# Decoder layer with product-key experts: dense blocks in another order, and the first eight expert groups' scores made ahead of the dense stage

## The chip, the core and the metric

The kernel is one program on one core of a Trainium2 chip. TensorE (PE) multiplies matrices into PSUM; VectorE (DVE), ScalarE (ACT) and GpSimd (POOL) work on SBUF tiles of 128 partitions; SyncE (SP) issues the plain transfers, POOL the gathers by index. Every engine works through its own instructions in a fixed order and waits on semaphores for the others. The time is the device time of one execution in microseconds (us); the median of three is quoted.

## The reference, cut to what matters

One decoder layer over 1024 tokens of 1024 features. The token mixers ahead of the feed-forward part are not touched by the change. What matters is the feed-forward part, a product-key layer with 16,384 experts of one row each: every token picks 16 of them in each of 8 heads.

```python
def peer_ffn(h, wq, k1, k2, u_tab, v_tab):
    q = (h @ wq)...                                  # 8 heads, two halves of 128
    s1, s2 = scores of the halves against 128 keys each
    v1, i1 = lax.top_k(s1, 16); v2, i2 = lax.top_k(s2, 16)
    top_s, pos = lax.top_k(sums of the pairs, 16)
    idx = i1 * 128 + i2 at pos                       # expert numbers
    gates = jax.nn.softmax(top_s, axis=-1)
    act = jax.nn.gelu(einsum('bthkd,btd', u_tab[idx], h))
    return einsum('bthk,bthkd->btd', gates * act, v_tab[idx])
...
h = layer_norm(ALPHA * h + peer_ffn(h) + sigmoid(h @ w_gate) * (p @ w_ple))
```

## The kernel before, in words

**Blocks.** The 1024 tokens are eight blocks of 128, worked on in three groups, `BLOCKS = [(0, 1), (2, 3, 4), (5, 6, 7)]`. The expert layer is computed in two ways. Blocks 0, 1, 2, 5 and 6 gather: for each of the 128 experts of a token POOL fetches a row of `u` and later one of `v` (128 rows, 512 KB, for the 128 tokens at a time) into one of six `vr` buffers, and DVE makes one product of it (class `Experts`; in the trace line L139, `vr<-vr,h1r` for `u`, `acc<-vr,w,acc` for `v`). That is 1,280 gathers and products in all. The blocks in `DENSE = (3, 4, 7)` are computed against all experts, in 128 groups of 128.

**The dense blocks.** `spread` turns the numbers and gates that `choose` found for one block into a table with a place for every expert: one-hot tiles `ohA` and `ohB` are made by DVE and ACT, four tokens at a time in 32 groups, PE multiplies them (L996), ACT copies the result into `stage`, and SP stores it in the DRAM table `Gd`. `dense` then takes the expert groups one by one. For each it needs two weight blocks of 512 KB, `uE` and `v`, which come through `stream` into eight buffers `wf`. `uE` is split by ACT and DVE into a high and a low half (`split`, tiles `hl`; DVE's part is L256), and PE makes the scores of three blocks, 384 columns, by 24 matmuls of halves (`mm`, L281 to L283: high by high, high by low, low by high, with `h1s` the split activations). ACT applies the Gelu and leaves `y` in one of seven buffers `cs`. DVE multiplies `y` by the gates in two halves (L1052), from tiles `gp` that SP loads from `Gd` for eight expert groups at a time, in two halves `c` of 768 KB (L1036): the 12 rows of `Gd` for a half are block after block, so `c = 0` is the first dense block and half of the second. Last, `back` (L1028) multiplies `y` by `v` and accumulates in six PSUM banks, `g` and `z`, over all expert groups; it is emitted one expert group behind the score.

**The order.** `main` emits the program by generators that tell how long each step takes, and `Merge` takes the one that is behind. In the last group of blocks `choose` of block 7, with its `spread`, is merged with `embed`; then `choose` of blocks 5 and 6 with `dense`. The gathers and their products are put between them at a rate. `choose` keeps its tables `top`, `cv` and `ci` in the same seven `cs` buffers as `y` and the one-hot tiles. From what is emitted a scheduler fixes each engine's instruction order when the program is built. On the chip each engine only follows it and waits.

```python
ex.rate = RATES["last"]
yield from Merge(choose(o, [t for t in o.tbs if t in DENSE]), embed(o))
ex.rate = RATES["dense"]
yield from Merge(choose(o, [t for t in o.tbs if t not in DENSE]), dense(h1s))
```

## Time and profile before

| | us |
|---|---|
| median of three runs | 3288.61 (3286.11 to 3297.98) |
| the profiled execution | 3287.69 |
| its span on the core | 3285.6 |
| PE busy | 2934.3 (89%) |
| DVE busy | 2626.9 (80%) |
| ACT busy | 1095.3 (33%) |
| POOL busy | 1581.4 (48%) |
| moved by the DMA engines | 1035.22 MB, mean 315 GB/s |

The profile records one execution: each instruction of each engine with its start and duration in us from the start of the span, the wait that came before it and what ended that wait, and the clock that was granted to PE in a stretch (1.0 is 2.4 GHz, 0.5 is 1.2 GHz). A row names the line of the kernel, the operation, and `out<-in` by the names of the tiles; `x8` is eight such instructions in a row. Matmuls are pipelined, so a row's duration reaches into the next one's. A whole fp32 matmul is two PE instructions in the trace, one row in an order of instructions.

### The profile page before, as it was taken

The page shows a single profiled execution, that of the slowest core. Times are in us where ns is not written, and L with a number is a line of the kernel's source. Part 1 is how long each engine was busy: PE and PEld are TensorE (multiplying, and loading weights), DVE is VectorE, ACT ScalarE, POOL GpSimd, SP SyncE. Part 2 cuts the span into 40 slices and gives each one's busy share as a digit, 9 for nine tenths or more (in the row PEclk, how much of TensorE's full clock was granted, in tenths as well). Part 3 has the DMA queues.
Part 4 walks back from the last instruction along what each step waited for, and adds up shares of the span by engine and source line. Part 5 has one row for each costly group of instructions (what it writes and reads, how often), then busy time and mean ns, then how long its engine had stood idle before and what let it go on. Part 6 is the DMA issues. An engine that isn't in the chain of part 4 may idle for free.

```text
span 3285.6 us, 39190 instructions
## 1 busy us (share of the span) xinstructions
PE 2934.3 (89%) x12265; PEld 2013.0 (61%) x12265; DVE 2626.9 (80%) x5567; ACT 1095.3 (33%) x2590; POOL 1581.4 (48%) x1313
## 2 busy tenths in 40 slices
PE   7997999969899937999898966999999999999990
PEld 6886655655464535667655554666666666666660
DVE  5535898788789999898887999976676677777788
ACT  5626335421621458556423154111111111111110
POOL 0000066667634544576674343545454555554564
PEclk9998999969999969999899988999999999999995
DMA  6344698989978979898899888999999999999997
GB/s 219 130 141 144 230 365 317 375 293 379 390 274 308 354 281 329 295 370 308 292 380 350 303 304 292 366 358 345 351 352 361 352 350 345 353 350 339 360 330 272
DMA packets 341824, 1035.22 MB, mean 315 GB/s; under 512 B 38512, under 2 KB 95216, under 8 KB 341616
## 3 DMA queue, kind: packets, MB, share of 16 engines
q0 software_dynamic: 184320, 671.17, 56.3%
q1 hardware_dynamic: 157296, 361.55, 30.3%
q8 instruction: 97, 1.59, 0.2%
q14 instruction: 111, 0.91, 0.1%
HBM read 991.17 MB, written 41.42 MB: 314 GB/s over the span
## 4 chain that ended last, share of the span: by engine, by line
PE 66%; DVE 15%; issue 7%; ACT 7%; DMA 3%; POOL 1%; SPq 0%; DVEq 0%; ACTq 0%; POOLq 0%
PE g L279 15%; PE g L1028 13%; PE z L1028 6%; PE m L283 5%; PE m L281 5%; PE m L282 5%; PE g L793 3%; DVE acc L139 3%; ACT ohB L161 2%; PE g L283 2%; PE g L281 2%; PE g L282 2%; PE m L617 2%; DVE vr L139 2%; PE z L590 1%
## 5 line engine op out<-in xcount | busy, mean ns | idle before, releaser
L1088 POOL DMA_INDIRECT vr<-in_u_dram,vidx x640 | 784.3, 1226 | 968.3 <-DVE V L139 385.7
L1088 POOL DMA_INDIRECT vr<-in_v_dram,vidx x640 | 793.4, 1240 | 706.9 <-DVE acc L139 297.6
L139 DVE SCALAR_TENSOR_TENSOR acc<-vr,w,acc 128x1024 f32<-128x1024 f32 x640 | 818.4, 1279 | 58.1 <-DMA vr<-in_v_dram,vidx 50.5
L139 DVE SCALAR_TENSOR_TENSOR vr<-vr,h1r 128x1024 f32<-128x1024 f32 x640 | 780.5, 1220 | 70.9 <-DMA vr<-in_u_dram,vidx 50.4
L1028 PE MATMUL g<-wf,y 128*128 128x512 f32 x1024 | 462.5, 594 | 16.6 <-DVE y L1052 16.6
L161 ACT ACTIVATE hl<-wf 128x512 fp32r<-128x512 f32 x256 | 161.7, 631 | 942.1 <-PE m L282 798.1
L256 DVE TENSOR_TENSOR hl<-wf,hl 128x512 fp32r<-128x512 f32 x256 | 178.9, 700 | 287.5 <-ACT hl L161 234.6
L281 PE MATMUL m<-h1s,hl 128*128 128x384 f32 x1024 | 393.8, 385 | 5.3 <-DVE gs L868 3.0
L283 PE MATMUL m<-h1s,hl 128*128 128x384 f32 x1024 | 347.7, 340 | 4.6 <-DVE hl L256 4.6
L282 PE MATMUL m<-h1s,hl 128*128 128x384 f32 x1024 | 345.6, 337 | 0.0
L279 PE MATMUL g<-hT,wf 128*128 128x384 f32 x1024 | 341.7, 489 | 3.2 <-DVE gs L860 3.2
L1028 PEld LDWEIGHTS g<-wf,y 128*128 128x128 f32 x1024 | 192.9, 190 | 203.8 <-issue 183.9
L279 PEld LDWEIGHTS g<-hT,wf 128*128 128x128 f32 x1024 | 192.4, 191 | 136.8 <-issue 9.8
L1028 PE MATMUL z<-wf,y 128*128 128x512 f32 x512 | 240.6, 592 | 0.0
L281 PEld LDWEIGHTS m<-h1s,hl 128*128 128x128 f32 x1024 | 193.8, 189 | 35.8 <-issue 29.7
L282 PEld LDWEIGHTS m<-h1s,hl 128*128 128x128 f32 x1024 | 193.8, 189 | 28.9 <-issue 28.9
L283 PEld LDWEIGHTS m<-h1s,hl 128*128 128x128 f32 x1024 | 193.5, 189 | 6.1 <-DVE hl L256 4.9
L996 PE MATMUL z<-ohA,ohB 128*128 128x128 f32 x768 | 137.2, 320 | 45.2 <-ACT ohB L161 19.6
L279 PE MATMUL g<-h1T,wf 128*128 128x384 f32 x512 | 173.0, 493 | 0.0
L1028 PEld LDWEIGHTS z<-wf,y 128*128 128x128 f32 x512 | 97.3, 190 | 122.4 <-issue 122.2
L996 PEld LDWEIGHTS z<-ohA,ohB 128*128 128x128 f32 x768 | 112.2, 211 | 71.8 <-ACT ohB L161 53.4
L256 DVE TENSOR_TENSOR wf<-wf 128x1024 fp32r<-128x1024 f32 x68 | 83.1, 1222 | 68.9 <-ACT wf L161 66.8
(336 smaller groups left out, 4606.5 us busy)
## 6 DMA issues: line engine op xcount, KB each, us to landing
wf<-in_uE_dram SPq DMA_DIRECT2D x128, 512.0 KB
wf<-in_v_dram SPq DMA_DIRECT2D x128, 512.0 KB
wf<-in_wmain_dram SPq DMA_DIRECT2D x84, 512.0 KB
wf<-in_wgate_dram SPq DMA_DIRECT2D x48, 512.0 KB
wf<-in_wq_dram SPq DMA_DIRECT2D x48, 512.0 KB
Gd<-stage SPq DMA_DIRECT2D x48, 512.0 KB
gp<-Gd SPq DMA_DIRECT2D x32, 768.0 KB
wf<-in_wout_dram SPq DMA_DIRECT2D x24, 512.0 KB
```

The source lines that it names most:

```text
L139: x = getattr(vec, op)(*args, **kw)
L161: x = nc.scalar.activation(o, i, f, **kw)
L256: vec.tensor_tensor(lo, src, hi, op=OP.subtract)
L279: pe.matmul(o, l[0], r[0], start=first, stop=last)
L281: pe.matmul(o, l[0], r[0], start=first, stop=False)
L282: pe.matmul(o, l[0], r[1], start=False, stop=False)
L283: pe.matmul(o, l[1], r[0], start=False, stop=last)
L617: pe.matmul(pw[:, c], sp[:, c], nident, start=False, stop=True, skip_group_check=True)
L793: pe.matmul(acc, yT[k // 4][:, k % 4, n * P:(n + 1) * P], wo[u][k // 2][:, k % 2, :], start=k == 0, stop=k == 7)
L996: pe.matmul(pg[:, k], B[:, k], A[:, k], start=True, stop=True)
L1028: pe.matmul(acc[d][c], y[:, d * P:(d + 1) * P], wv[:, c * 512:(c + 1) * 512], start=e == 0, stop=e == P - 1)
L1088: pool.indirect_dma_start(out=vr, out_offset=None, in_=use[0], in_offset=bass.IndirectOffsetOnAxis(ap=idx[:, s:s + 1], axis=0))
```

## The change

`DENSE` becomes `(7, 3, 4)`, so that the three dense blocks are contiguous columns (256 to 640) of the tile with the unsplit activations, `h1Ts`. A new generator `ahead` follows `embed`, and is thereby merged with `choose` and `spread` of block 7: for the first `NPRE = 8` expert groups it makes the scores by eight whole fp32 matmuls each, from the unsplit `uE` and `h1Ts`, and its Gelu goes into two buffers of four scores each (`yp`, one of the eight `c6` tiles, and a tile of the kind `vx`), in which they stay until `dense` multiplies them by the gates. `dense` makes its own scores from the ninth group on, split as before. The stream is ordered accordingly: eight `uE` unsplit, their eight `v`, then pairs. The `gp` tiles are taken when they are loaded, and the load for the groups 8 to 15 is taken apart: half 0 at the first group, half 1 at the fifth. In the new order of the dense blocks half 0 of the gates is block 7 and half of block 3, and half 1 the rest of block 3 and block 4.

```diff
@@ -64,7 +64,10 @@
 
 
 BLOCKS = [(0, 1), (2, 3, 4), (5, 6, 7)]
-DENSE = (3, 4, 7)
+DENSE = (7, 3, 4)
+
+DCOL = 256
+NPRE = 8
 OFF = (0, 256, 0)
 HOTS = "DAAD"
 RATES = {"mix": 1.0, "branch": 1.0, "keys": 1.0, "choose": 1.0, "last": 1.0, "dense": 1.0}
@@ -447,7 +450,9 @@
             q["ple"].append((planned("wpg", (u,), i in FASTQ)[0], planned("wple", (u,))[0]))
         plan.append(q)
     experts = [(a["uE"][e], a["v"][e * P:(e + 1) * P, :]) for e in range(P)]
-    stream.items += [(x, i == 0) for e in experts for i, x in enumerate(e)]
+    stream.items += [(x, False) for x, _ in experts[:NPRE]]
+    for e, (u, v) in enumerate(experts):
+        stream.items += [(u, True), (v, False)] if e >= NPRE else [(v, False)]
 
     class Blk:
         pass
@@ -1015,11 +1020,25 @@
                 split(slot(tb)[:, 4 * q:4 * q + 4, :], *[t[:, :, c] for t in r[q]])
         return r
 
-    def dense(h1s):
+    def ahead(ys):
+
+        h = h1Ts[:, :, DCOL:DCOL + ND * P]
+        for e in range(NPRE):
+            if e % 4 == 0:
+                y = c6("yp") if e == 0 else T([P, 4, 387], F32, "vx", 1)[:, :, :W]
+            wu = stream.get(experts[e][0])[0]
+            pu = PT("m")
+            for k in range(8):
+                pe.matmul(pu[:, :W], wu[:, k, :], h[:, k, :], start=k == 0, stop=k == 7)
+            ys.append(y[:, e % 4, :])
+            act.activation(ys[e], pu[:, :W], AF.Gelu)
+            yield 5.2
+
+    def dense(h1s, ys):
 
         w = ND * P
         acc = [[PT("g"), PT("g")], [PT("g"), PT("g")], [PT("z"), PT("z")]]
-        gp = [[c6("gp", (P, 4 * ND, 8, 16)) for _ in range(2)] for _ in range(2)]
+        gp = [[None, None], [None, None]]
         todo = []
 
         def back(e, y, wv):
@@ -1028,32 +1047,41 @@
                     pe.matmul(acc[d][c], y[:, d * P:(d + 1) * P], wv[:, c * 512:(c + 1) * 512],
                               start=e == 0, stop=e == P - 1)
 
-        def load(e):
+        def load(e, cs=(0, 1)):
             if e < P:
                 i, k = divmod(e, 64)
                 src = Gd[:, :, i, :, k:k + 8, :].rearrange("d q p i t -> p (d q) i t")
-                for c in range(2):
+                for c in cs:
+                    gp[e // 8 % 2][c] = c6("gp", (P, 4 * ND, 8, 16))
                     dma.dma_start(gp[e // 8 % 2][c], src[:, 4 * ND * c:4 * ND * (c + 1)])
 
-        load(0)
-        for e in range(P):
-            if e % 8 == 0:
-                load(e + 8)
+        def score(e):
             wu = stream.get(experts[e][0])
-            wv = stream.get(experts[e][1])[0]
             pu = PT("m")
             for k in range(8):
                 i, j = divmod(k, 4)
                 mm(pu[:, :w], [t[:, j, :] for t in wu[i]], [t[:, j, :] for t in h1s[i]], k == 0, k == 7)
             y = csel("y")[:, :w]
             act.activation(y, pu[:, :w], AF.Gelu)
+            return y
+
+        load(0)
+        for e in range(P):
+            if e == 0:
+                load(8, (0,))
+            elif e == 4:
+                load(8, (1,))
+            elif e % 8 == 0:
+                load(e + 8)
+            y = score(e) if e >= NPRE else ys[e]
+            wv = stream.get(experts[e][1])[0]
             y3 = y.rearrange("p (c a t) -> p c a t", c=2, t=16)
             for c in range(2):
                 vec.tensor_tensor(y3[:, c], y3[:, c], gp[e // 8 % 2][c][:, :, e % 8, :], op=OP.mult)
             todo.append((e, y, wv))
             if len(todo) > 1:
                 back(*todo.pop(0))
-            yield 9.2
+            yield 9.2 if e >= NPRE else 5.2
         back(*todo.pop(0))
         g, b = ln2
         hs = []
@@ -1167,9 +1195,10 @@
                 h1s = halve()
                 yield from keys(o)
                 ex.rate = RATES["last"]
-                yield from Merge(choose(o, [t for t in o.tbs if t in DENSE]), embed(o))
+                ys = []
+                yield from Merge(choose(o, [t for t in o.tbs if t in DENSE]), chain(embed(o), ahead(ys)))
                 ex.rate = RATES["dense"]
-                yield from Merge(choose(o, [t for t in o.tbs if t not in DENSE]), dense(h1s))
+                yield from Merge(choose(o, [t for t in o.tbs if t not in DENSE]), dense(h1s, ys))
 
     now = bg = 0.0
     for c in main():
```

**PE around the spread of block 7.** `m` is PSUM for scores, `self` and `gt` are the chosen experts' numbers and gates of the block, transposed as the spread begins. The kernel before has 48 matmuls of halves, two expert groups, directly ahead of these rows:

```order
L283 MATMUL m<-h1s,hl 128x384
L974 MATMUL z<-ident,self 128x128
L975 MATMUL z<-ident,self 128x128
L976 MATMUL z<-ident,gt 128x128
L996 MATMUL z<-ohA,ohB 128x128 x125
L281 MATMUL m<-h1s,hl 128x384
L282 MATMUL m<-h1s,hl 128x384
```

The changed kernel, from the last transposes of `embed` on:

```order
L751 MATMUL m<-ident,h1T 128x128 x8
L1032 MATMUL m<-h1T,wf 128x384 x38
L979 MATMUL z<-ident,self 128x128
L980 MATMUL z<-ident,self 128x128
L981 MATMUL z<-ident,gt 128x128
L1032 MATMUL m<-h1T,wf 128x384 x10
L1001 MATMUL z<-ohA,ohB 128x128 x2
L1032 MATMUL m<-h1T,wf 128x384 x3
L1001 MATMUL z<-ohA,ohB 128x128 x6
L1032 MATMUL m<-h1T,wf 128x384 x9
L1001 MATMUL z<-ohA,ohB 128x128 x8
L1032 MATMUL m<-h1T,wf 128x384 x4
```

All 64 whole matmuls stand ahead of the fifth group of the spread, 38 of them ahead of its transposes; 112 one-hot matmuls and then eight `back` matmuls follow these rows.

**SP at the end of the spread.** `h1r` is the activation row of a block whose gathers begin. Before:

```order
L1106 DMA h1r<-h1d 128x1024
L260 DMA wf<-in_v_dram 128x1024
L260 DMA wf<-in_uE_dram 128x1024
L260 DMA wf<-in_v_dram 128x1024
L1002 DMA Gd<-stage 128x1024 x16
L1036 DMA gp<-Gd 128x12x128 x3
L260 DMA wf<-in_uE_dram 128x1024
L260 DMA wf<-in_v_dram 128x1024
```

After:

```order
L1134 DMA h1r<-h1d 128x1024
L263 DMA wf<-in_v_dram 128x1024 x7
L1007 DMA Gd<-stage 128x1024 x2
L263 DMA wf<-in_v_dram 128x1024
L1007 DMA Gd<-stage 128x1024 x14
L1056 DMA gp<-Gd 128x12x128 x5
L263 DMA wf<-in_uE_dram 128x1024
L263 DMA wf<-in_v_dram 128x1024
L263 DMA wf<-in_uE_dram 128x1024
L263 DMA wf<-in_v_dram 128x1024
L1056 DMA gp<-Gd 128x12x128
```

All loads of `v` for the first eight groups now come ahead of the last stores of the table, and every load of gates after them; before, a load of half 0 stood far ahead of these rows. The fourth and fifth load of gates wait for DVE's gated products of the first groups.

**DVE at the first gated scores.** Before (`ci`, `cv`, `pos` and `top` are tables of `choose` for blocks 5 and 6):

```order
L139 TENSOR_TENSOR ci<-top 128x8
L139 MAX_INDEX pos<-top,cv 128x8
L139 TENSOR_TENSOR ci<-top 128x8x2
L1052 TENSOR_TENSOR y<-y,gp 128x192 x3
L139 MAX_INDEX pos<-top,cv 128x8
L139 TENSOR_TENSOR ci<-top 128x8x4
L256 TENSOR_TENSOR hl<-wf,hl 128x512
L139 SCALAR_TENSOR_TENSOR acc<-vr,w,acc 128x1024
```

After:

```order
L142 TENSOR_TENSOR ci<-top 128x8
L1080 TENSOR_TENSOR yp<-yp,gp 128x192 x3
L142 MAX_INDEX pos<-top,cv 128x8
L142 TENSOR_TENSOR ci<-top 128x8x2
L1080 TENSOR_TENSOR yp<-yp,gp 128x192
L1080 TENSOR_TENSOR vx<-vx,gp 128x192
L142 MAX_INDEX pos<-top,cv 128x8
L142 SCALAR_TENSOR_TENSOR acc<-vr,w,acc 128x1024
L142 TENSOR_TENSOR ci<-top 128x8x4
L142 TENSOR_TENSOR ci<-top 128x8 x2
L1080 TENSOR_TENSOR yp<-yp,gp 128x192 x2
```

Before, 96 rows follow the three products until the next gated product; after, the 16 products of the first eight groups lie within 22 rows of the order. In DVE's whole order 46 gather products stand behind the last gated score after, and 45 before.

## Rows read from the trace of the kernel before

**Rows 1.** Windows: from:to, us, PE, PEld, DVE, ACT, POOL busy, PEclk, DMA share, GB/s

```profile
1770.00:1934.00 164.00, 141.49 (x499) 86.48 (x497) 163.96 (x588) 28.73 (x56) 66.07 (x62) 0.93 0.86 307
1934.00:1999.00 65.00, 51.98 (x279) 41.28 (x280) 65.00 (x145) 62.00 (x193) 22.32 (x22) 0.95 0.89 300
1999.00:2053.00 54.00, 31.90 (x120) 21.50 (x118) 48.53 (x197) 11.18 (x18) 19.50 (x17) 0.84 0.85 285
2053.00:3205.00 1152.00, 1152.00 (x4420) 791.78 (x4420) 842.79 (x1316) 200.00 (x366) 608.56 (x483) 1.00 0.96 351
...
3220.00:3240.00 20.00, 0.00 (x0) 0.00 (x0) 17.86 (x15) 0.00 (x0) 16.04 (x14) 0.50 0.97 360
```

**Rows 2.** Timeline of PE in the dense stage: start, us, line, operation, count [wait <-releaser]

```profile
2105.21 3.59 PE L1028 MATMUL g<-wf,y 128*128 128x512 f32 x8
2108.64 1.88 PE L1028 MATMUL z<-wf,y 128*128 128x512 f32 x4
...
3194.87 3.59 PE L1028 MATMUL g<-wf,y 128*128 128x512 f32 x8
```

**Rows 3.** Groups of DVE, 2200 to 3100: count | busy, mean ns | idle before <-releasers

```profile
L139 DVE SCALAR_TENSOR_TENSOR acc<-vr,w,acc 128x1024 f32<-128x1024 f32 x163 | 208.8, 1281 | 3.7 <-DMA vr<-in_v_dram,vidx 1.1
L256 DVE TENSOR_TENSOR hl<-wf,hl 128x512 fp32r<-128x512 f32 x192 | 135.0, 703 | 248.1 <-ACT hl L161 206.0 <-issue 24.1 <-PE m L283 15.5
```

**Rows 4.** Timeline of DVE from the last gated score to the layer norm

```profile
3196.55 0.62 DVE L1052 TENSOR_TENSOR y<-y,gp 128x192 f32<-128x192 f32 x2
...
3258.88 5.25 DVE L139 SCALAR_TENSOR_TENSOR acc<-vr,w,acc 128x1024 f32<-128x1024 f32 x4 [0.42 <-DMA vr<-in_v_dram,vidx]
```

**Rows 5.** Timeline of PE, 2050 to 2062

```profile
2052.89 5.58 PE L1028 MATMUL g<-wf,y 128*128 128x512 f32 x8 [14.24 <-DVE y L1052]
```

**Rows 6.** Timeline of ACT, 1997 to 2066

```profile
1998.93 0.66 ACT L173 ACTIVATE stage<-z 128x256 f32<-128x256 f32 x2 [1.78 <-PE z L996]
...
2021.98 0.63 ACT L161 ACTIVATE hl<-wf 128x512 fp32r<-128x512 f32 x1 [16.18 <-DVE ci L139]
...
2062.53 0.31 ACT L168 ACTIVATE gt<-gt 128x128 f32<-128x128 f32 x1 [25.03 <-DVE gt L139]
```

**Rows 7.** Timeline of PE: sixteen whole matmuls (another stage), then the last spread

```profile
1769.10 5.33 PE L279 MATMUL g<-h1T,wf 128*128 128x384 f32 x16
...
1910.81 0.69 PE L281 MATMUL m<-h1s,hl 128*128 128x384 f32 x1 [3.04 <-DVE gs L868]
...
1916.74 0.36 PE L281 MATMUL m<-h1s,hl 128*128 128x384 f32 x1
...
1931.98 0.47 PE L974 MATMUL z<-ident,self 128*128 128x128 f32 x1 [9.85 <-DVE self L971]
...
1935.35 6.70 PE L996 MATMUL z<-ohA,ohB 128*128 128x128 f32 x34 [2.48 <-DVE ohB L994]
...
1946.68 1.02 PE L996 MATMUL z<-ohA,ohB 128*128 128x128 f32 x6 [0.19 <-ACT ohB L161]
...
1948.57 1.02 PE L996 MATMUL z<-ohA,ohB 128*128 128x128 f32 x6 [0.19 <-ACT ohB L161]
```

**Rows 8.** Timeline of DVE, 2010 to 2030

```profile
2012.81 0.90 DVE L1052 TENSOR_TENSOR y<-y,gp 128x192 f32<-128x192 f32 x3 [3.19 <-DMA gp<-Gd]
...
2024.26 0.29 DVE L139 TENSOR_REDUCE sm<-gt 128x8 f32<-128x128 f32 x1 [2.28 <-ACT gt L168]
```

**Rows 9.** The chain of work that ended last, 1990 to 2070: start, us, what

```profile
1999.34 3.96 DMA Gd<-stage
2003.39 9.40 DMA gp<-Gd
...
2017.00 7.39 DMA wf<-in_v_dram
```

**Rows 10.** Timeline of DVE, 2096 to 2101

```profile
2099.24 0.35 DVE L1052 TENSOR_TENSOR y<-y,gp 128x192 f32<-128x192 f32 x1
```

## The prediction

> **What bounds the kernel now.** I read the table of windows first. From 2053 us to 3205 us TensorE (PE) is busy for all of 1152 us, at full clock [rows 1]. One expert group there takes 9.313 us: the `back` of expert group 9 (they count from 0) starts at 2105.21 and that of group 126 at 3194.87, so 1089.66 us lie between 117 of them [rows 2]. VectorE (DVE) works beside it with gaps, and the gaps are waits for the split copies of ScalarE (ACT), 206 us, against 1.1 us for gathered rows [rows 3]. ACT makes those copies when PE hands it buffers back, so DVE is led by PE there, and the gather products of blocks 5 and 6 stand at fixed places between DVE's other work. After the last gated score (3196.55) the trace has 45 such products left; the last four start at 3258.88 and end at 3264.13, so 1.5 us each, and the layer norm follows to the end of the span, 3285.6 [rows 4]. So the end is one line of 9.313 us a group and then a fixed tail: whatever moves the start of that line moves the end by as much, as long as the number of products left at the line's end is the same.
>
> What sets the start of the line? From 1934 to 1999 ACT is busy 62.00 of 65 us and DVE 65.00: the gates of the last dense block are spread there. From 1999 to 2053 PE does 31.90 of 54 us [rows 1]. It waits 14.24 us there for a gated score [rows 5], while ACT waits 16.18 and 25.03 us for tables of block 5 and 6 [rows 6], whose buffers (`cs`) the scores share. That is the stretch that can be won, and the change fills a part of it.
>
> **The change part by part.**
>
> **Work moved.** A whole score is 16 instructions, 5.33 us [rows 7]. A split one is 24; a `back` has 8 + 4 instructions, the four start 3.43 us after the eight [rows 2], so 12 take 5.15 us and the split score the rest, 9.31 - 5.15 = 4.16 us, 0.173 an instruction. The change adds 8 x 5.33 = 42.6 us on PE before the line and takes 8 x 4.16 = 33.3 us out of it. DVE loses 16 subtractions of 0.7 us [rows 3], 11 us, and ACT as many copies. In the line both lie beside PE's work, in engines that wait (248 us before such subtractions alone [rows 3]); I count them as nothing by themselves, and the few that fall ahead of the line are in the count of rows below.
>
> **When the spread ends.** PE's first score of the last stage starts at 1910.81, released by DVE [rows 7]; DVE's rows ahead of that are the same before and after, so I take 1911 again. 38 matmuls (0.666 us each, two instructions) then stand ahead of the three transposes that open the spread: 25.3 us. PE was at half clock at first: 18 split matmuls took from 1910.81 to 1916.74, 0.33 us each, where 0.173 is the pitch of the line [rows 7]; 5.9 us at about half the pace cost 2.7 us more. So the transposes come at 1938.8 where they came at 1931.98. Then 26 more whole matmuls, 17.3 us, run between the first four groups of one-hot products, 4 x 1.58 us = 6.3 (34 instructions in 6.70 us are 4.25 groups), with 0.9 for the transposes: 1963.3 is where `ahead` ends. The other 28 groups go at the pace that ACT sets, 1.89 us (from 1946.68 to 1948.57 [rows 7]): 52.9 us, to 2016.2. While PE is late ACT can prepare groups ahead, as far as the `cs` buffers go; I take two of 1.89 us, 4 us: 2012.2. By DVE alone it would be earlier: first one-hot at 1940 (DVE has the indices at 1931.9 [rows 7], and then 7 gather products in the place of 3), 32 groups of 1.12 us and 24 products of 1.2 us, to 2005. The last copy of the spread ended at 1999.6 [rows 6], so the spread ends 12.6 us later. The PE time is placed beside the spread, but it is not hidden by it.
>
> **From there to the first gated score.** The last copy, the store, the load of the gates: the product came at 2012.81 [rows 8], 13.2 us after, 3.96 and 9.40 us of it the two transfers [rows 9]. The same again gives 2025.4, say 2026. Half of the gates was there early before (columns of blocks 3 and 4 only); now both halves are loaded at the end. I take no cost for that here; rival D prices it.
>
> **From the first gated score on.** Two bounds. PE alone: eight `back`s, three split scores and two more `back`s precede that of group 10, and PE starts at half clock, which made the first eight instructions 5.58 instead of 3.59 us [rows 5]: 2026 + 41.2 + 12.5 + 10.3 + 2 = 2092. Before, group 10 would be at 2105.21 + 9.31 = 2114.5, so this is 22.5 us earlier. DVE: by the two orders, 186 rows lead from the first gated products to those of group 10 (numbered 11th), 20 of them gather products. In the kernel before it is 196 rows with 32, from 2012.81 to 2099.51, 86.7 us [rows 8, 10]; with 2.28 us of waiting [rows 8] and 1.2 us a product (its row reads 1.28, of which the end lies beside the next [rows 3]) 164 rows took 46 us, 0.281 each. Now: 20 x 1.2 + 166 x 0.281 + 2 x 2.28 (two tables of ACT, since the choice for blocks 5 and 6 is the same work) = 75.2 us, to 2101. The later of the two bounds decides: the `back` of group 10 at 2101 instead of 2114.5, which as a line is 2008 + 9.31 n against 2021.4 + 9.31 n, 13.4 us earlier. I take that, since DVE was what PE waited for in this stretch. The other ends: 22.5 us if DVE's rows cost less, and about nothing if PE stays behind DVE by as much as it did before (the product of 2099.24 was used 15 us later).
>
> **At the end.** The order has 46 gather products behind the last gated score where it had 45: +1.5 us. The layer norm is the same.
>
> **Transfers.** SP now asks for eight scores' weights first, then eight `v`, then the gates; five loads of gates stand in a row, of which the fourth and fifth wait for gated scores of the first eight groups, with the next two weights behind them. Those weights are first needed some 41 us later (eight `back`s), and a load took 7.39 us there [rows 9], so I cost that wait at nothing; without that cover it would cost one load, 7 us. Six more weight blocks (3.1 MB) and 14 more gathered rows (7.3 MB) must land by the end of the spread. It is 12.6 us later, worth 4.4 MB at 351 GB/s, and in the stretch before the DMA engines were 0.86 and 0.89 busy against 0.97 at best [rows 1], worth 23 us or some 8 MB. It fits, with little over.
>
> Sum: -13.4 + 1.5 = -11.9 us on the profiled 3287.69 us, 3275.8 us; against the median, 3288.61, that is 0.38% less. That execution lies 0.9 us below the median, so I make no other correction. What a measurement of this kernel can tell from no change is 0.5%, 16.4 us: below 3272 is faster, above 3305 slower.
>
> **The rivals.**
>
> A: only PE bounds the start of the line. DVE's rows there hold about 20 us of short operations that wait on nothing PE needs; if the order's places cost less than mine, the line starts 21 to 22.5 us earlier, less 1.5: 3267. For it: PE's 14.24 us wait is the largest of its waits there [rows 5]. Against it: DVE was busy 48.53 of those 54 us [rows 1].
>
> B: transfers decide. In the line the DMA engines are 0.96 busy with 351 GB/s, at best 0.97 with 360 [rows 1]. If the 10.4 MB do not fit ahead, gathered rows come late, DVE's fixed order holds the gates back, or the products left over make the tail longer. The gain is then given back, and 3284 to 3288 comes out.
>
> C, the slower side: the whole scores run starved or at half clock. One mechanism: PE waits for each of the eight weight blocks of 512 KB behind gathers and so stays at the lower clock, where the instruction pitch was 0.33 against 0.173 us, nearly double [rows 2, 7]. 64 matmuls then take 85 instead of 43 us. The DMA engines were 0.89 busy beside the spread [rows 1], which speaks for it; that eight buffers let the loads run ahead of PE speaks against. The whole line moves with it: it loses once `ahead` ends over 13 us after 1963, loses more than the 0.5% from 30 us on, and at 42 us gives 3305 to 3317.
>
> D: both halves of the gates come one after the other. The second is needed now for the first product; 0.786 MB at half of 351 GB/s is 4.5 us: 3280. The Trainium skill (DMA: Bandwidth & Descriptors, Queues, rings and completion order) states that each DMA engine takes the queues that have work by turns, packet by packet, and works off one queue's descriptors in their order; by that rule this 4.5 us (my estimate) comes out, since the gathers run on another queue. The trace shows three gate loads landing within the 9.40 us of one [rows 9], which does not tell them apart.
>
> **How the numbers follow.** Forecast 0.50 (its own range 3268 to 3284; three tenths of it, 0.15, below 3272), A 0.19, B 0.12, D 0.08, C 0.11. Faster by over 0.5%: 0.15 + 0.19 = 0.34. Slower: C, 0.11. Within 0.5%: the rest, 0.55. The predicted time is the forecast's, 3276. The range has to reach A's 3267 and a little beyond for its own spread, 3264, and B's 3288 with a little for a tail that grows, 3292; what is left out is C and a few hundredths below 3264.
>
> **What would show it.** The first whole score at 1911, in its first 6 us at half clock; the three transposes at 1939 (C: after 1950); the last copy of the spread at 2012; the first gated product at 2026 (D: 2030); PE full from the eighth `back` on and the `back` of group n at 2008 + 9.31 n (A: 1999, B: 2021); no wait of 14 us for a gated score, and ACT's waits of 16 and 25 us gone; 46 gather products of 1.5 us after the last gated score. I am wrong if the number of products left at the line's end changes, if the line is longer than 9.31 us a group, or if DVE waits for gathered rows in it.

## The result, and the profile after

The changed kernel takes 3267.02 us (median of five runs, 3264.65 to 3273.81) where the kernel before takes 3288.71 (five runs, 3286.11 to 3297.98): a ratio of 0.9935, 95% interval 0.9923 to 0.9948, 21.7 us. The forecast was 3276, with a range of 3264 to 3292; rival A had named 3267. The profiled execution took 3266.96 us, its span is 3265.2. The ratios here and below are to executions of the kernel before that were measured beside each kernel, and their intervals are some 3 to 6 us wide to either side, so a few us between two medians of the changed kernels are not clear of noise by themselves.

The windows of the changed kernel (the columns are those of [rows 1]):

```profile
1934.00:1999.00 65.00, 55.61 (x286) 40.38 (x285) 63.58 (x117) 57.37 (x181) 28.19 (x26) 1.00 0.95 353
1999.00:2053.00 54.00, 34.02 (x92) 16.49 (x92) 48.40 (x168) 11.11 (x26) 11.73 (x12) 0.81 0.89 287
2053.00:3185.00 1132.00, 1131.55 (x4353) 778.76 (x4351) 829.20 (x1359) 198.03 (x361) 597.02 (x477) 1.00 0.97 352
3185.00:3266.00 81.00, 0.00 (x0) 0.00 (x0) 71.22 (x93) 0.00 (x0) 39.56 (x35) 0.52 0.73 272
```

The dense stretch is the same picture as before, PE busy for all of it, and it ends 20 us earlier. The stretch from 1934 to 1999 has changed: 353 GB/s where [rows 1] had 300. PE's timeline, from the scores made ahead to the end of the line:

```profile
1907.80 26.46 PE L1032 MATMUL m<-h1T,wf 128*128 128x384 f32 x76 [2.39 <-ACT h1p L176]
1934.09 0.27 PE L979 MATMUL z<-ident,self 128*128 128x128 f32 x1
...
2023.73 8.88 PE L1047 MATMUL g<-wf,yp 128*128 128x512 f32 x16 [19.22 <-DVE yp L1080]
2032.44 1.88 PE L1047 MATMUL g<-wf,vx 128*128 128x512 f32 x4
2034.16 1.88 PE L1047 MATMUL g<-wf,yp 128*128 128x512 f32 x4
2035.88 1.88 PE L1047 MATMUL z<-wf,yp 128*128 128x512 f32 x4
...
2075.11 3.59 PE L1047 MATMUL g<-wf,y 128*128 128x512 f32 x8
...
2084.43 3.59 PE L1047 MATMUL g<-wf,y 128*128 128x512 f32 x8
...
2093.74 3.59 PE L1047 MATMUL g<-wf,y 128*128 128x512 f32 x8
...
3174.09 3.59 PE L1047 MATMUL g<-wf,y 128*128 128x512 f32 x8
```

76 instructions are the 38 whole matmuls ahead of the transposes. The eight `back`s on scores that were made ahead follow from 2023.73; 2075.11, 2084.43 and 2093.74 are the `back`s of groups 8, 9 and 10 and 3174.09 is that of group 126, so 1098.98 us for 118 groups, 9.313 again, a line of 2000.6 + 9.313 n against 2021.4 before. DVE's timeline at the first gated products, at those of groups 9 and 10, at the last ones and at the last gather product (before: [rows 4, 8, 10]):

```profile
2023.32 0.90 DVE L1080 TENSOR_TENSOR yp<-yp,gp 128x192 f32<-128x192 f32 x3 [5.33 <-DMA gp<-Gd]
...
2026.94 0.63 DVE L1080 TENSOR_TENSOR yp<-yp,gp 128x192 f32<-128x192 f32 x2 [0.28 <-DMA gp<-Gd]
...
2081.93 0.62 DVE L1080 TENSOR_TENSOR y<-y,gp 128x192 f32<-128x192 f32 x2
...
2090.11 0.62 DVE L1080 TENSOR_TENSOR y<-y,gp 128x192 f32<-128x192 f32 x2
...
3175.31 0.62 DVE L1080 TENSOR_TENSOR y<-y,gp 128x192 f32<-128x192 f32 x2
...
3237.17 6.57 DVE L142 SCALAR_TENSOR_TENSOR acc<-vr,w,acc 128x1024 f32<-128x1024 f32 x5 [0.15 <-DMA vr<-in_v_dram,vidx]
```

From the last gated score to the end of the gather products are 68.4 us (67.6 before), for 46 products (45), and the layer norm takes its 21.4 us. So the line starts 20.8 us earlier, the tail is 0.9 us longer, and the layer norm is the same: 20 us, as the span shows.

ACT's timeline from the last copy of the spread, and the chain of work that ended last (before: [rows 6, 9]):

```profile
2004.54 0.66 ACT L176 ACTIVATE stage<-z 128x256 f32<-128x256 f32 x2 [0.27 <-PE z L1001]
...
2033.63 0.31 ACT L171 ACTIVATE gt<-gt 128x128 f32<-128x128 f32 x1 [27.13 <-DVE gt L142]
...
2063.74 0.64 ACT L164 ACTIVATE hl<-wf 128x512 fp32r<-128x512 f32 x1 [14.66 <-DVE ci L142]
```

```profile
2004.95 6.19 DMA Gd<-stage
2011.21 12.08 DMA gp<-Gd
2023.32 0.37 DVE yp L1080
```

ACT still waits as long as before for the tables of blocks 5 and 6, but the gated scores of the first eight groups no longer stand behind those tables. PE waits longer for its first gated score than before, 19.22 us. What that wait is worth, the run with late `v` below shows: its first gated products came 3.8 us earlier, its last `back` ended 2.4 us earlier, and the gather products ended at the same time.

### The profile page after: what moved, and what is told of

It is laid out like the page before. It is cut to its first block, busy times and chain, and to the rows that moved or that the text cites. A ratio compares the mean times of both kernels' runs of the same rounds, so it can differ in the third digit from the quotient of the medians.

```text
span 3265.2 us, 39000 instructions
## 1 busy us (share of the span) xinstructions
PE 2928.7 (90%) x12201; PEld 1994.7 (61%) x12201; DVE 2616.4 (80%) x5551; ACT 1086.9 (33%) x2574; POOL 1571.5 (48%) x1313
## 4 chain that ended last, share of the span: by engine, by line
PE 66%; DVE 16%; issue 7%; ACT 7%; DMA 4%; POOL 1%; SPq 0%; DVEq 0%; POOLq 0%; ACTq 0%
PE g L282 14%; PE g L1047 13%; PE z L1047 7%; PE m L286 5%; PE m L284 5%; PE m L285 5%; DVE acc L142 3%; PE g L798 3%; ACT ohB L164 2%; DVE vr L142 2%; PE g L286 2%; PE g L284 2%; PE g L285 2%; PE m L622 1%; PE m L1032 1%
## 5 line engine op out<-in xcount | busy, mean ns | idle before, releaser
L164 ACT ACTIVATE hl<-wf 128x512 fp32r<-128x512 f32 x240 | 151.2, 631 | 909.9 <-PE m L285 779.0
L1047 PE MATMUL g<-wf,y 128*128 128x512 f32 x960 | 431.3, 592 | 0.0
L259 DVE TENSOR_TENSOR hl<-wf,hl 128x512 fp32r<-128x512 f32 x240 | 167.7, 699 | 285.9 <-ACT hl L164 247.5
L284 PE MATMUL m<-h1s,hl 128*128 128x384 f32 x960 | 370.3, 386 | 0.0
L286 PE MATMUL m<-h1s,hl 128*128 128x384 f32 x960 | 322.9, 336 | 0.0
L285 PE MATMUL m<-h1s,hl 128*128 128x384 f32 x960 | 322.2, 336 | 0.0
L1047 PEld LDWEIGHTS g<-wf,y 128*128 128x128 f32 x960 | 180.3, 189 | 173.0 <-issue 172.1
L1047 PE MATMUL z<-wf,y 128*128 128x512 f32 x480 | 225.5, 592 | 0.0
L285 PEld LDWEIGHTS m<-h1s,hl 128*128 128x128 f32 x960 | 180.6, 188 | 28.7 <-issue 28.7
L284 PEld LDWEIGHTS m<-h1s,hl 128*128 128x128 f32 x960 | 180.6, 188 | 28.7 <-issue 28.7
L286 PEld LDWEIGHTS m<-h1s,hl 128*128 128x128 f32 x960 | 180.3, 188 | 0.0
```

The costliest lines, as they stand in the source:

```text
L164: x = nc.scalar.activation(o, i, f, **kw)
L259: vec.tensor_tensor(lo, src, hi, op=OP.subtract)
L284: pe.matmul(o, l[0], r[0], start=first, stop=False)
L285: pe.matmul(o, l[0], r[1], start=False, stop=False)
L286: pe.matmul(o, l[1], r[0], start=False, stop=last)
L1047: pe.matmul(acc[d][c], y[:, d * P:(d + 1) * P], wv[:, c * 512:(c + 1) * 512], start=e == 0, stop=e == P - 1)
```

## The experiments

By its trace the result looks like rival A: PE's own work sets the line, and the end follows. The experiments were to show which part of the change moves the line, and whether the end really is "line and fixed tail" (the tail is what follows the last gated score: the gather products that are left, and the layer norm). One table holds what the traces show (the first attempt at extra bytes, which came late from its first transfers on, is left out of it). The products done by 2110 us are counted in the groups of DVE from the start of the span to that point, of 1280; the gated halves likewise, of 256 (two for each expert group); the MB are those that the DMA view gives for the same stretch; the last columns are the end of the last gather product (the start of the layer norm) in the profiled execution, and the median of the runs. In the run with early gates half 1 of the first eight scores was multiplied from 1918.0 on; the table gives the first product of half 0.

| kernel | first gated score | last `back` ends | products, gated halves by 2110 | MB by 2110 | products end | median |
|---|---|---|---|---|---|---|
| before | see [rows 8] | 3205.3 | 780, 22 | 629.0 | 3264.2 | 3288.71 |
| changed | 2023.3 | 3184.5 | 788, 26 | 635.9 | 3243.8 | 3267.02 |
| reorder alone | 2015.2 | 3204.6 | 783, 22 | 630.6 | 3259.2 | 3282.47 |
| own buffers | 2009.7 | 3188.9 | 782, 24 | 632.2 | 3254.5 | 3275.79 |
| split ahead | 2018.9 | 3182.8 | 782, 26 | 632.2 | 3251.3 | 3274.45 |
| four ahead | 2013.1 | 3184.3 | 784, 26 | 634.4 | 3251.3 | 3274.53 |
| 8 more products | 2023.6 | 3192.6 | 787, 26 | 634.8 | 3245.0 | 3268.13 |
| own buffers, bound | 2010.8 | 3190.7 | 781, 24 | 631.7 | 3254.0 | 3275.87 |
| split ahead, bound | 2019.1 | 3186.0 | 782, 26 | 632.1 | 3250.1 | 3271.70 |
| fewer bytes | 2017.0 | 3178.7 | 790, 26 | 637.5 | 3218.0 | 3245.25 |
| extra bytes in the line | 2026.1 | 3191.4 | 785, 24 | 634.9 | 3256.3 | 3275.82 |
| late v | 2019.5 | 3182.1 | 788, 26 | 636.4 | 3243.9 | 3269.08 |
| early gates | 2023.1 | 3182.0 | 783, 28 | 634.5 | 3246.2 | 3267.80 |

### Which part moves the line

**The reorder alone.** The edit on the changed kernel:

```diff
-NPRE = 8
+NPRE = 0
```

> The changed kernel without the scores made ahead: the dense blocks are in the new order and the gates are loaded as in the changed kernel, but all 128 scores are made in the dense stage, split, in the shared buffers. The order has 43 gather products behind the last gated score (45 before, 46 in the changed kernel). Theory (PE bounds the line of 9.31 us a group, what moved ahead of it is the gain): both halves of the gates come late, so the first gated score is some 5 us later than before, the line starts at 2021 to 2026, and 2 products fewer give 3 us back: 3285 to 3291 us. Rival (the new order of the blocks by itself brings part of the gain): under 3280.

Measured: 3282.47 us, a ratio to the kernel before of 0.9984 (0.9974 to 0.9993). The last `back` ends 0.7 us earlier than before and PE still waits 13.15 us for a gated score, so the line has not moved. The end came 5 us earlier, more than the 3 expected, and the median lies between the theory's 3285 to 3291 and the rival's under 3280. With both halves of the gates loaded at the end the line was no later.

**Own buffers.** On top of the reorder alone:

```diff
-            y = csel("y")[:, :w]
+            if e < 8:
+                if e % 4 == 0:
+                    own[0] = c6("yp") if e == 0 else T([P, 4, 387], F32, "vx", 1)[:, :, :W]
+                y = own[0][:, e % 4, :]
+            else:
+                y = csel("y")[:, :w]
```

> As the reorder alone, but the first eight scores (still split, still made in the dense stage) go into the two buffers of four that the changed kernel gives them, and not into the buffers shared with the tables of blocks 5 and 6. The order has 50 gather products behind the last gated score, 4 more than the changed kernel. Theory (the gain is the PE work placed ahead of the first gated score): PE can only begin most of these scores after the spread, and the splits stand in DVE's order between the choices of blocks 5 and 6: the line starts near 2012, end 3284 us. Rival (the shared buffers were what held PE back, and freeing them is enough): PE works through from the end of the spread, the line starts at 2000 to 2004, and with the 4 products, 6 us, the end is 3273 to 3277.

Measured: 3275.79, ratio 0.9971 (0.9956 to 0.9987). The rival was right: the last `back` ends 16.4 us earlier than before, 15.7 us earlier than with the reorder alone, although nothing is made ahead; the long wait for a gated score is gone, and the largest wait on PE from 1990 on is 2.55 us. The end gained only 4.7 us of that. The buffers shared with the tables of blocks 5 and 6 were what held PE back.

**Split scores ahead.**

```diff
-    stream.items += [(x, False) for x, _ in experts[:NPRE]]
+    stream.items += [(x, True) for x, _ in experts[:NPRE]]
...
-                pe.matmul(pu[:, :W], wu[:, k, :], h[:, k, :], start=k == 0, stop=k == 7)
+                i, j = divmod(k, 4)
+                mm(pu[:, :W], [t[:, j, :] for t in wu[i]], [t[:, j, :] for t in h1s[i]], k == 0, k == 7)
```

> As the changed kernel, but the eight scores made ahead are made of split operands (24 matmuls, 4.16 us each, instead of 16 in 5.33). The order has 52 gather products behind the last gated score, 6 more than the changed kernel: 9 us. Theory (ACT and DVE set the pace of the spread, so whole operands are worth their 9 us of PE): 16 copies and subtractions more put 10 us on ACT and 11 on DVE beside the spread, the last copy of the spread comes at 2008 to 2015 instead of 2005, the line starts 3 to 10 us later, end 3279 to 3286. Rival (PE time ahead of the spread is what counts): the spread ends some 9 us earlier, the line with it, end near 3267.

Measured: 3274.45, ratio 0.9962 (0.9948 to 0.9976). Neither forecast came true. The spread ended at 2003.2, 2 us earlier, where the theory had 3 to 10 later and the rival 9 earlier, and the line's last `back` 1.7 us earlier. On PE's side the splits cost nothing. And yet the end came 7.4 us later than in the changed kernel. DVE's groups from 1770 to 2060, before, changed and here, show what whole operands are worth:

```profile
L139 DVE SCALAR_TENSOR_TENSOR acc<-vr,w,acc 128x1024 f32<-128x1024 f32 x104 | 132.4, 1273 | 0.0
L256 DVE TENSOR_TENSOR hl<-wf,hl 128x512 fp32r<-128x512 f32 x16 | 10.7, 678 | 0.0
```

```profile
L142 DVE SCALAR_TENSOR_TENSOR acc<-vr,w,acc 128x1024 f32<-128x1024 f32 x109 | 138.9, 1274 | 1.2 <-DMA vr<-in_v_dram,vidx 0.9
L259 DVE TENSOR_TENSOR hl<-wf,hl 128x512 fp32r<-128x512 f32 x4 | 2.7, 680 | 0.0
```

```profile
L142 DVE SCALAR_TENSOR_TENSOR acc<-vr,w,acc 128x1024 f32<-128x1024 f32 x103 | 131.0, 1272 | 0.0
L259 DVE TENSOR_TENSOR hl<-wf,hl 128x512 fp32r<-128x512 f32 x20 | 13.5, 681 | 1.9 <-ACT hl L164 1.9
```

DVE is busy there for nearly the whole time (284.49 of 290 us before). Twelve subtractions less, 8 us, are room for gather products: 109 against 104, and 103 with splits. That time is won on the engine that is full there, not on PE. That it is the whole of the 7.4 us is an argument from these rows; no run changed DVE's time alone.

**Four ahead.** The edit is `NPRE = 4`.

> As the changed kernel with four expert groups ahead instead of eight. The order has 50 gather products behind the last gated score, 4 more than the changed kernel: 6 us. Theory (PE alone sets the line from the first gated score on: its start is the first gated score + 2 - 4.16 us for each score beyond two that is made ahead): the spread ends at 2000 to 2005, the first gated score comes at 2018, the line starts at 2018 + 2 - 8 = 2012, end near 3285. Rival (what counts is only that the first gated scores have buffers of their own, four are enough): the line starts at 2000 as with eight, end 3273.

Measured: 3274.53, ratio 0.9964 (0.9950 to 0.9978). The line's last `back` ends at 3184.3, as with eight: the rival again. The end is 7.5 us later than with eight.

So three kernels have the line of the changed kernel to within 5 us, and each ends 7 to 9 us behind it. "Line and fixed tail" explained that only by the count of products behind the last gated score, 50 to 52 instead of 46. The next three runs bind that count.

### Whether the count of products at the end is the cause

The binding, here for the run with 8 more products (all other bound runs have 435 in place of 443, which leaves 46 products):

```diff
+                x = vec.tensor_tensor(y3[:, c], y3[:, c], gp[e // 8 % 2][c][:, :, e % 8, :], op=OP.mult)
+            if e >= 16:
+                k = 799 + round((e - 16) * (443 / 111))
+                if k <= len(prods):
+                    order(x, prods[k - 1])
...
+            prods.append(f(vr))
```

> As the changed kernel, with DVE's order bound so that 8 more gather products stand evenly between the gated scores of groups 16 to 127: 38 are left behind the last one instead of 46. Theory (the end is the line's start, 127 groups of 9.31 us and some 1.45 us for each product left, and the transfers can follow): the line starts at 2000.6 as before, 11.5 us less behind it, end 3255 us. Rival (the DMA engines, 0.97 busy in the line, set the pace of the gathers): DVE waits for gathered rows in the line, a group takes over 9.31 us, and the end stays within 3 us of 3267.

> As the run with own buffers for the first eight scores (split, made in the dense stage, nothing made ahead), with DVE's order bound so that 46 gather products are left behind the last gated score, as in the changed kernel, instead of 50. Theory (that run differs from the changed kernel by the line's start, 2005.0 against 2000.6, and by 4 products more at the end): 4.4 us behind the changed kernel, 3271. Rival (its longer end comes from transfers that fell behind, not from the order): 3275 as without the binding, with waits for gathered rows in the line.

> As the run with split scores made ahead, with DVE's order bound so that 46 gather products are left behind the last gated score instead of 52. Theory (whole or split makes no difference to the line, which started at 1998.8 against 2000.6; the rest was the 6 products more at the end): 3265, level with the changed kernel. Rival (the 16 splits more on ACT and DVE cost their 10 us somewhere): 3272 and over.

Measured: 3268.13 with 8 more products in the line (ratio 0.9942, 0.9925 to 0.9959), where the theory said 3255; 3275.87 for own buffers with 46 left (0.9959, 0.9945 to 0.9973), where it was 3275.79 with 50; 3271.70 for split scores with 46 left (0.9945, 0.9928 to 0.9962) where it was 3274.45 with 52. The theory fell in all three by the medians, which lie within 3 us of the unbound kernels; the interval of the first run excludes it clearly, in the other two it lies at the edge of the interval. The traces say the same: the gather products end within 1.2 us of where they ended unbound. Products that are moved from the tail into the line come back as a longer line (the last `back` ends 1.8 to 8.1 us later). PE at the end of the run with 8 more:

```profile
3177.18 1.98 PE L1047 MATMUL g<-wf,y 128*128 128x512 f32 x4 [0.35 <-DVE y L1080]
...
3182.60 1.98 PE L1047 MATMUL g<-wf,y 128*128 128x512 f32 x4 [1.72 <-DVE y L1080]
...
3188.93 1.98 PE L1047 MATMUL g<-wf,y 128*128 128x512 f32 x4 [2.63 <-DVE y L1080]
```

By 3000 us that kernel had done 1152 products, as many as the changed kernel, but 215 gated halves where that had 218: the order asked for more products and got the same number, and gated scores waited for them, as the rival had it. The gathers have a pace of their own. The changed kernel itself was not run with its own count bound.

### Whether that pace is the transfers'

**Fewer bytes.**

```diff
+        keep = [] if e >= 16 and e % 8 == 1 else [(v, False)]
+        stream.items += [(u, True)] + keep if e >= NPRE else keep
...
+            wv = wv if e >= 16 and e % 8 == 1 else stream.get(experts[e][1])[0]
```

> As the changed kernel, but 14 of the expert groups from 16 on (each eighth) multiply back with the block of v of the group before instead of loading their own: 7.3 MB of loads are left out, and so the right weights of these groups; PE, DVE and ACT do the same work. The order now has 14 gather products more in the line, 32 instead of 46 behind the last gated score, so the line moves as many bytes as in the changed kernel. Theory (transfers): the line is not slower than in the changed kernel, last gated score at 3175, 14 products less behind it, end 3247. Rival (the run with 8 products more in the line lost its gain to the places of the products in DVE's order, not to bytes): the line slips by 8.5 us or more, as there, end 3256 to 3266.

Measured: 3245.25, ratio 0.9874 (0.9858 to 0.9891); the theory had 3247, the rival 3256 to 3266. The first and last gated scores:

```profile
2016.96 0.90 DVE L1082 TENSOR_TENSOR yp<-yp,gp 128x192 f32<-128x192 f32 x3 [1.66 <-DMA gp<-Gd]
...
3169.34 0.62 DVE L1082 TENSOR_TENSOR y<-y,gp 128x192 f32<-128x192 f32 x2
```

Between them lie 1152.4 us; in the changed kernel 1152.0. 14 more products stand between them, and the line is not longer by a microsecond; with 8 more and no bytes less it was 1164.9. From 2024 to 3176 the DMA engines moved 350 GB/s here and 349 in the changed kernel: gathers took the place of the loads that were left out. 21.8 us for 7.3 MB is about the full price, 21 us at the 352 GB/s of the dense stretch. So it is bytes, not places in DVE's order, that decide how many products the line holds.

**Extra bytes.** The opposite, 16 copies of 512 KB that nothing waits for. The first attempt did not do what it should:

```diff
+            if e % 7 == 6 and e < 112:
+                dma.dma_start(spare[e // 7], experts[e][1])
```

> As the changed kernel, with 16 copies of a weight block (512 KB, 8.4 MB in all) from DRAM to a spare place in DRAM, one after every seventh expert group of the dense stage; nothing waits for them, PE, DVE and ACT do the same work in the same order, 46 gather products are left behind the last gated score. Theory now (transfers: at 353 GB/s the end comes when the bytes are moved, and the changed kernel ends earlier because by 2110 us it had moved 6.9 MB more than the kernel before): the line slips or the tail grows, 8.4 MB / 353 GB/s = 24 us, end 3291. Rival (PE's line of 9.31 us a group and a fixed tail; the engines that move data have room in it): 3267 to 3270.

Measured: 3287.10, 20 us behind the changed kernel, but SP's timeline shows where the copies went:

```profile
17.52 4.40 SPq L1083 DMA_DIRECT2D spare<-in_v_dram  x6
23.89 0.50 SPq L1083 DMA_DIRECT2D spare<-in_v_dram  x1
26.91 5.74 SPq L1083 DMA_DIRECT2D spare<-in_v_dram  x4
34.69 7.34 SPq L1083 DMA_DIRECT2D spare<-in_v_dram  x5
```

With nothing to hold them back they were placed among the first transfers of the program, where the first weights waited for them, and the whole kernel came late. It says nothing on the line. In the second attempt each copy is bound behind the last weight load:

```diff
+                order(dma.dma_start(spare[e // 7], experts[e][1]), last[0])
```

> The run with extra bytes again, mended: there the 16 copies had moved to the program's first transfers, since nothing held them back. Now each is bound behind the last weight load asked for before it, one every seventh expert group of the dense stage, 8.4 MB in all, and DVE's order is bound so that 46 gather products are left behind the last gated score, as in the changed kernel. Theory (transfers, 353 GB/s): up to the first gated score all as in the changed kernel; the last gated score is up to 24 us later, end 3285 to 3291. Rival (PE's line has room beside it for 8.4 MB in 1,180 us, 2%): 3267 to 3270.

Measured: 3275.82, ratio 0.9967 (0.9958 to 0.9977), between the two: 8.8 us for 8.4 MB, where the full price would be 24 and the rival's 0 to 3. The DMA view from 2700 to 3160, changed kernel and this one:

```profile
DMA packets 57159, 159.72 MB, mean 347 GB/s; under 512 B 4784, under 2 KB 20144, under 8 KB 57132
```

```profile
DMA packets 58209, 165.56 MB, mean 360 GB/s; under 512 B 4975, under 2 KB 20335, under 8 KB 58102
```

In this last part of the line the DMA engines could take 360 GB/s, 3 to 4% more. That holds for this part alone. The windows from 2110 to 2700, changed kernel and this one:

```profile
2110.00:2700.00 590.00, 590.00 (x2286) 408.53 (x2285) 414.38 (x675) 105.21 (x193) 304.80 (x244) 1.00 0.98 355
```

```profile
2110.00:2700.00 590.00, 590.00 (x2301) 411.10 (x2300) 405.96 (x667) 103.47 (x192) 296.64 (x238) 1.00 0.97 356
```

Nine of the 16 copies were issued there, the rate stayed the same, and 238 gather products were done instead of 244: where the copies went (4.7 MB), 3.1 MB of gathers were not. Only from 2700 on, where the other kernels move 347 to 351 GB/s, did this one catch up a part. Why those move less there, and so why bytes taken away gave their full price and bytes added only a part, is not settled; one reading is that the gathers (six buffers, POOL, a transfer, DVE, in turn) cannot use that room. It was only argued, not tried.

### Whether it is bytes moved beside the spread

> As the changed kernel, but the v blocks of groups 4 to 7 are loaded behind the first gates and not beside the spread: 2.1 MB less are moved by 2000 us. They are first needed some 20 us after the first gated score. DVE's order is bound so that 46 gather products are left at the end. Theory (what the change wins is bytes moved beside the spread): 2.1 MB / 353 GB/s = 6 us, end 3273. Rival (the score's work moved ahead on PE is what counts, the v blocks come in time): 3267.

```diff
+        x = dma.dma_start(wf, ap)
+        if gate and len(gate) < 5:
+            order(x, gate[0])
+            gate.append(x)
```

Measured: 3269.08, ratio 0.9951 (0.9933 to 0.9969), 2 us behind the changed kernel and inside the spread of its runs; the theory had 3273. The interval of the ratio holds both forecasts, so the time does not decide between them; the trace says more, since the products end at 3243.9 as in the changed kernel (3243.8). By 2000 us 1.5 MB less had been moved than in the changed kernel (598.24 against 599.75), by 2060 it was 1.8 MB more (619.42 against 617.61), and by 2110 products and gated halves were the same. So the bytes that were left out beside the spread were made up before the line, and nothing was lost by it that the trace shows. It fits the reading that what matters is how much is done when DVE's full stretch ends, near 2110; it does not prove it.

### The gates

> As the changed kernel, but the second half of the first gates (blocks 3 and 4, known long before) is loaded ahead of the last stage, and the gates of groups 8 to 15 are loaded behind the weights of group 8, so that one load of gates stands behind the spread instead of three; DVE's order is bound so that 46 gather products are left behind the last gated score, as in the changed kernel. Theory (DVE is busy without a gap from the first gated score to about 2082 us, so its wait of 5.6 us for gates is what can be won): first gated score at 2017 to 2019, line 3 to 5.6 us earlier, end 3261 to 3264. Rival 1 (PE sets the line by the eight scores that it multiplies back first): the line moves by all of the first gated score's shift, 5 to 7 us, 3260 to 3262. Rival 2 (what is gained there is lost to transfers in the same stretch): 3267.

```diff
+                g1 = half(0, 1)
...
-        load(0)
+        load(0, (0,))
...
-                load(8, (0,))
-            elif e == 4:
-                load(8, (1,))
+                pass
+            elif e == 6:
+                load(8)
```

Measured: 3267.80, ratio 0.9932 (0.9915 to 0.9948): rival 2's time, no gain, though the interval of the ratio holds the theory's 3261 to 3264 too. The reason is neither the theory's nor the rival's: the first products of half 0 came at 2023.1, as in the changed kernel (2023.3). The chain of this run:

```profile
2006.98 5.26 DMA Gd<-stage
2012.31 10.75 DMA gp<-Gd
```

With a single load of gates behind the spread that load still took 10.75 us; with three the first of them took 12.08 in the changed kernel and 10.01 in the run with late `v`. The half that was fetched early had not been what the first product waited for: in the changed kernel DVE waited 5.33 us for half 0 and 0.28 us for half 1.

## Why the prediction was right, and where it was not

The direction was right and the time lies in the range, at its lower part; by the prediction's own 0.5% the change is faster (0.65%), which had 0.34 against 0.55 for "within". Step by step:

- **The start of `ahead` and the spread.** First whole score forecast at 1911, measured 1907.80; transposes 1938.8, measured 1934.09; last copy of the spread 2012, measured 2005.2. Some 3 us are an earlier start. Most of the rest is the term for the first four groups of one-hot products: between whole matmuls their 32 instructions cost 3.6 us and not 6.3. PE was at half clock for less (granted clock 0.50 from 1904 to 1908, 0.97 from 1911 to 1915): the first 76 instructions took 26.3 us, the next 20 came 0.323 us apart (1934.42 to 1940.87), so it cost 1.7 us where 2.7 were counted. ACT's pace of 1.89 us held.
- **From the copy to the first gated score**: 18.1 us where 13.2 were taken. The store took 6.19 us instead of 3.96, the first load of gates 12.08 instead of 9.40. Together that is about as much as rival D's 4.5 us, but by accident. D took it that the first product needs both halves. In the changed kernel's order it does not: PE's first 16 and 4 instructions, ahead of any in `z`, are four from each of five scores, the part of block 7, which half 0 gates; and DVE's wait for half 1 was 0.28 us. D's mechanism itself is there, beside the path: loads issued together land one after the other. In the run with late `v` the first products of the two halves waited for their loads until 2019.48 and 2024.71, 5.2 us apart:

```profile
2019.48 0.90 DVE L1087 TENSOR_TENSOR yp<-yp,gp 128x192 f32<-128x192 f32 x3 [3.41 <-DMA gp<-Gd]
...
2024.71 0.63 DVE L1087 TENSOR_TENSOR yp<-yp,gp 128x192 f32<-128x192 f32 x2 [1.89 <-DMA gp<-Gd]
```

In the reorder alone they came 3.9 us apart (2015.23 and 2019.16), with own buffers 6.6 (2009.71 and 2016.32), and in the changed kernel 3.6. Of the rule of the Trainium skill that stood beside D (DMA: Bandwidth & Descriptors, Queues, rings and completion order: queues by turns, one queue's descriptors in their order), the traces agree with the second part, and 3.6 to 6.6 us lie around the 4.5 worked out by it. The prediction's sentence that three loads landed within the 9.40 us of one was a misreading: from 2003.3 to 2012.82 SP's queue moved 1.46 MB in the kernel before, and three loads are 2.36 MB.

- **The step that failed is DVE's bound for group 10.** Forecast 75.2 us after the first gated products, to 2101; measured 66.8, to 2090.11. Two terms were too large: the two waits of 2.28 us for ACT's tables do not exist in the changed kernel, 4.6 us, and the short rows cost 0.258 us each ((66.8 - 20 x 1.2) / 166) instead of 0.281, 3.8 us. Without that bound PE's own work set the line, 2000.6 against 1999 for rival A. It was close: gated products of group 9 started at 2081.93 and were used at 2084.43, and in the run with split scores PE waited 1.66 us for them.
- **PE's own bound was miscounted, and A's start was hit by luck.** The sum for PE, 2092, has three split scores ahead of the `back` of group 10. A `back` is emitted one group behind its score, so four stand there (groups 8 to 11): 4.16 us more, 2096, and for A a line that starts at 2003 instead of 1999. Measured were 2093.74, because the first gated product came 2.7 us earlier than the forecast 2026. From PE's start at 2023.73 to 2093.74 are 70.0 us, and the sum with four scores is 70.1.
- **The tail**: 46 products and 0.9 us more, forecast 1.5.
- **Two signs were wrong.** PE's wait for a gated score is not gone but longer (19.22 us), and ACT's waits of 16 and 25 us are now 14.66 and 27.13. The forecast read them as the loss itself. What was lost before was that gated scores stood behind the tables, and the run with own buffers shows it: against the reorder alone it has 15.7 us of the line's 20.8.
- **"One line and a fixed tail" is only half of it.** It gave the right sum here, since the tail stayed as it was. But the line is held from two sides: PE is busy for all of it, and the gathers go at the pace of the transfers. The dense stretch begins with a backlog, and the end is when that is worked off. By 2110 us the changed kernel had done 8 products (4.2 MB) and two expert groups (2 x 1.24 MB) more than the kernel before, 6.7 MB by that count and 6.85 by the DMA view:

```profile
DMA packets 195677, 629.04 MB, mean 298 GB/s; under 512 B 26332, under 2 KB 43100, under 8 KB 195533
```

```profile
DMA packets 197563, 635.89 MB, mean 301 GB/s; under 512 B 26545, under 2 KB 43313, under 8 KB 197418
```

6.85 MB at 352 GB/s are 19.5 us, and the last product ended 20.4 us earlier. For the other nine kernels without added or omitted bytes the same account, from the MB by 2110 and 352 GB/s, counted from the changed kernel, comes within 4.4 us of the products' end. That is agreement over a spread of 15 us and not an experiment; the experiments show that the line's pace is the transfers' (fewer bytes). Rival B named the transfers, but as what takes the gain away; they are also the measure of it. The prediction's sentence that the bytes fit, with little over, was right.

What each part is worth, by the medians: the new order of the blocks 6 us, the buffers of their own 7 more, and making eight scores ahead from whole operands 9 more. The ratios put them at 5, 4 and 12, and the intervals of the first two steps overlap. The new order moved no line; by 2110 us it had moved 1.6 MB more, 4.4 us by the account above, and why is open. Of the last part the whole operands are 7.4 us, or 4.7 with the count bound, where the intervals overlap; that it is DVE's time is argued from its rows. The 43 us of PE work that were moved ahead matter least: with four ahead, eight or none the line ended within 5 us.

No kernel of these beats the changed one, apart from the one that leaves weights out.

## What to carry to other kernels

When a wait's name is "engine X for engine Y's tile", look whose buffers that tile comes from before counting work: here 16 us of a line hung on seven buffers that two streams of work shared, though the end gained only 5 of them. Where one stretch is full on one engine and the next is full on another and on the transfers, price an edit by how much of the next stretch's backlog it lets the first one work off, on the engine that is full there (here subtractions on DVE), not by the work it moves on the engine that waits; these kernels fit that, and no run tried it alone. A count of instructions left at the end can be an effect: here it was bound, and the time stayed within 3 us. And when a rival's time comes true to the microsecond, redo its steps all the same: here two errors of its sum, 4.2 us and 2.7 us, went in opposite directions.

## What the runs showed of the hardware

The first load of gates, 768 KB in pieces of 512 bytes, took 10 to 12 us whether one or three were issued together (10.75, 10.01, 12.08), and the second of those issued together landed 3.6 to 6.6 us after the first. In the dense stretch the DMA engines showed a busy share of 0.97 at 352 GB/s, and from 2700 to 3160 they showed 0.96 both at 347 GB/s and, with copies of whole blocks added, at 360: a busy share near 1 did not mean that nothing more could be moved. From 2110 to 2700 it was 0.98 and 0.97 at 355 and 356, and there the added copies did not raise the rate; fewer rows were gathered.
